# The lo parts of the attention weights made on GpSimd instead of VectorE, in a two-layer decoder step

## The chip, the cores and the metric

The kernel runs on one core of a Trainium2 chip. TensorE multiplies matrices, VectorE and ScalarE work element by element, GpSimd (POOL in the profile) is a further engine that here issues some DMAs, and SyncE issues most DMAs. Each engine takes its instructions in order from its own queue; engines wait for each other by semaphores. The metric is the time of one execution on the device, in microseconds, lower is better.

## The reference, cut to what matters

One step of a two-layer decoder for a prompt of 512 tokens and 8 single-token samples, model width 1024. Layer 0 mixes by pooling, layer 1 by attention within a window of 128 keys. Each layer has a gated feed-forward block before and after its mixer. All is float32. The part that the change touches is the mixer of layer 1:

```python
q = _rope((h @ w_q[j]).reshape(B, T, N_KV_HEADS, GROUP, HEAD_DIM), pos)
out = _window_attention(q, kk, vv, wb, pos0, attn_sinks[j]) @ w_o[j]
x = x + out
```

w_q and w_o are 1024 x 1024. The attention takes softmax over two blocks of 128 keys with a learned sink per head, for 16 heads of 64 and 4 key heads.

## The kernel before

**Split products.** TensorE is fed a rounded format (fp32r) here, and to keep float32 accuracy every operand is written as hi + lo: hi is the operand rounded, lo is what is missing. A product is three matmuls: hi x hi, hi x lo, lo x hi (terms, L410; mm, L413). The tokens are the moving side: 520 columns, as two halves of 260. A weight tile is loaded for each matmul.

**Weight stream.** The class Weights (L97) holds a list of chunks (1 MB loads into the tile raw, three buffers) and of pieces (views of a chunk, mostly 128 x 4 x 128, that is 512 elements a partition). _split (L180) makes a piece ready: ScalarE copies it into wh with rounding (L194), VectorE subtracts to get wl (L195), each from a ring of six buffers. get takes the next piece, prefetch makes pieces up to five ahead of the last one taken, and loads chunks up to two ahead. A raw buffer is free again when the last piece read from it has its wh and wl.

The list for layer 1's mixer is 16 query pieces (four chunks, L305 to L322) and 16 output pieces (four chunks, L323 to L337); numbered 0 to 31 below. The query pieces are views with a gap every 64 elements, the output pieces of 128. The next feed-forward block's pieces follow.

**Attention.** A table of cosines and sines, csq, is loaded into a raw buffer, from ScalarE's queue (L1036, L1037). For each of 8 tiles t of the query, q_part multiplies two pieces; q_evac (L1056) then ropes the result on VectorE (L919 to L923: a product with the cosines, a shuffle, a product with the sines, a sum), and splits it. 16 units (t and half) follow: scores on TensorE, the masked maximum (L1101) and small steps on VectorE, exponentials on ScalarE (L1121), scaling by the denominator on both (L1134, L1136), transposes (L1146) and their split (L245, L246), and the product with the values (L1169). The loop at L1313 interleaves the units with the query products of later tiles, and from turn 12 with the first half of the output product (o_part, L1278), whose second half follows at L1340. load_values (L1294) loads the cached values of the samples into a raw buffer, vc, and writes the samples' own value row into it by a DMA from GpSimd's queue (L1297).

**GpSimd here.** Its queue has the two memsets of qz at the start (L1042), and the DMA of L1297. In the feed-forward blocks it issues accumulating DMAs (L158, L159).

**Order.** Instructions are written in the order of the program text, and the order on each engine is then made by a planner, which runs the program in a timeline of estimated durations (L1449); instructions wrapped in later keep their place relative to each other.

Of the kernel before, what the change touches and what calls it, by code (L numbers as in the profile page):

```python
# [11 lines left out]
F32 = mybir.dt.float32  # L12
# [3 lines left out]
ALU = mybir.AluOpType  # L16
# [80 lines left out]
class Weights:  # L97
# [4 lines left out]
    def __init__(self, nc, rawp, splp, chunks_ahead, ahead):  # L102
        self.nc, self.rawp, self.splp = nc, rawp, splp
        self.ca, self.ahead = chunks_ahead, ahead
        self.chunks, self.items = [], []
        self.nl = self.na = self.ns = self.ng = 0
        self.late = None
        self.pin = lambda ins: ins

    def chunk(self, *dmas):  # L110
        self.chunks.append([list(dmas), None, None])
        return len(self.chunks) - 1
# [67 lines left out]
    def _split(self, i):  # L180
        nc = self.nc
        while self.ns <= min(i, len(self.items) - 1):
            it = self.items[self.ns]
            self.load(it[0])
            self.add_up(it[0])
            src = it[1](self.chunks[it[0]][1])
            n = src.shape[1]
            wh = self.splp.tile([P, 4, P], F32R, tag="wh", name="wh")
            wl = self.splp.tile([P, 4, P], F32R, tag="wl", name="wl")
            dh, dl = wh[:, :n, :], wl[:, :n, :]  # L190
            if len(src.shape) == 4:
                dh = dh.rearrange("p k (e d) -> p k e d", e=2)
                dl = dl.rearrange("p k (e d) -> p k e d", e=2)
            self.pin(nc.scalar.activation(dh, src, AF.Copy))  # L194
            self.pin(nc.vector.tensor_tensor(dl, src, dh.bitcast(F32), op=ALU.subtract))  # L195
            it[2] = (wh, wl)
            held = any(c < it[0] for c, _, _ in self.items[self.ns + 1 : self.ns + 3])
            self.load(it[0] + self.ca - held)
            self.add_up(it[0] + 1)
            self.ns += 1  # L200
# [12 lines left out]
def yoco_step(ctx, tc, ins, outs):  # L213
    nc = tc.nc
# [20 lines left out]
    def pair(tags, shape, dtype=F32R):  # L235

        return tuple(big.tile(shape, dtype, tag=t, name=t) for t in tags)
# [3 lines left out]
    def split(dst, src, scale=None):  # L241

        hi, lo = dst
        if scale is None:
            S.activation(hi, src, AF.Copy)  # L245
            V.tensor_tensor(lo, src, hi.bitcast(F32), op=ALU.subtract)  # L246
        else:
            S.activation(hi, src, AF.Copy, scale=scale)
            V.scalar_tensor_tensor(lo, src, scale, hi.bitcast(F32), op0=ALU.mult, op1=ALU.subtract)

    def later(ins):

        return tc.keep_in_program_order(ins)


    W = Weights(nc, rawp, splp, 2, 5)
# [93 lines left out]
    def gcol(n, k):  # L350
        return gT[:, n * 8 + k : n * 8 + k + 1]
# [12 lines left out]
    def square(k, pool, tag, order=lambda ins: ins):  # L364
        sq = pool.tile([P, TOK], F32, tag=tag, name="sq", bufs=1 if tag == "rp0" else 2)
        S.activation(sq, x[k], AF.Square)
        if k == 0:
            order(V.tensor_copy(acc[:, :TOK], sq))
        else:
            order(V.tensor_tensor(acc[:, :TOK], acc[:, :TOK], sq, op=ALU.add))  # L370
# [259 lines left out]
    def deferred(n, tmp, tag, tags, lst, w=TOK):  # L630


        def f(k):
            z = pair(tags, [P, w])
            split(tuple(a[:, :TOK] for a in z), x[k], gcol(n, k))
            lst.append(z)
            square(k, tmp, tag)

        return f
# [393 lines left out]
    with tc.tile_pool(name="at", bufs=2) as at:  # L1033
# [152 lines left out]
        def q_part(t, h):  # L1186
            if h == 0:
                qb[t] = duo()
            q_half(qb[t], 4 * h)

        later(S.activation(warm, ones[:, 0:1], AF.Exp))
        for h in (0, 1):
            q_part(0, h)
        qq[0] = q_evac(0, qb[0])
# [78 lines left out]
        def o_samples(t):  # L1273
            split(tuple(a[:, SP:TOK] for a in mov5[t]), oS[:, t, :])
# [38 lines left out]
        for n in range(2 * KT + VLAG):  # L1313
# [21 lines left out]
            if n == 13:  # L1335
                for t in range(len(mov5)):
                    o_samples(t)
        later(S.activation(warm, ones[:, 0:1], AF.Silu))
        after_o = deferred(5, at, "rp0", XX, mov6)
        for m in range(KT):  # L1340
            o_part(m, 4, after=after_o)
# [111 lines left out]
```

## Time and profile before

| what | us |
|---|---|
| median of 3 runs (1691.66 to 1692.97) | 1692.24 |
| the profiled execution, its time | 1691.85 |
| its span | 1690.0 |
| query products begin on TensorE | 1143.0 |
| first masked maximum on VectorE | 1163.1 |
| last value product on TensorE ends | 1294.6 |

From 1143 to 1296, busy time of single groups on the engines that share the work:

| engine, line, work | count | us |
|---|---|---|
| ScalarE L1121 exponentials, with reads of their sums | 64 | 49.7 |
| ScalarE L194 wh | 25 | 15.5 |
| ScalarE L1134 scaling | 32 | 14.4 |
| VectorE L1101 masked maximum, with reads of it | 64 | 29.3 |
| VectorE L246 lo of the transposed probabilities (from PSUM) | 32 | 19.7 |
| VectorE L195 wl | 25 | 17.1 |
| VectorE L920, L922, L923 rope products and sum | 24 | 16.7 |
| VectorE L1136 scaling | 32 | 9.8 |

A row of instruction groups gives the line, engine, operation, out and in tiles with their shapes, the count, and then busy time and the mean of one in ns; after a second bar the idle time of the engine just before them, and what ended it. A row in order of time gives start, duration, engine, line, and in brackets the idle time before it with its releaser. On VectorE an instruction's last part overlaps the next one's start, so the busy times add up to a little more than the time they take.

### The profile page before, as it was taken

The numbers are of one execution on the slowest core, as the hardware profiler recorded it, in microseconds if no ns is written. First come the engines' busy times: TensorE is split into PE (matmuls) and PEld (weight loads), VectorE is DVE, ScalarE is ACT, GpSimd is POOL, SyncE is SP. The second block draws the span as 40 slices with busy tenths as digits, with TensorE's granted clock in tenths as the row PEclk, the third lists the DMA queues.
The fourth block names the chain that finished last, engine by engine and source line by source line (L and its number), as shares of the span: only waits on it lengthen the run. The fifth ranks groups of instructions, "written<-read, shape, count | busy, mean of one in ns | idle before, by whom it ended". The sixth has DMA issues, their size and how long they took to land.

```text
span 1690.0 us, 34449 instructions
## 1 busy us (share of the span) xinstructions
PE 1657.5 (98%) x13754; PEld 1642.7 (97%) x13754; DVE 1254.4 (74%) x2452; ACT 903.5 (53%) x1793; POOL 142.3 (8%) x176
## 2 busy tenths in 40 slices
PE   9999999999999999999999999999989999999997
PEld 8999999999999999999999999998879999999996
DVE  6866866887875875888775875888876885785776
ACT  6743643665652652656552652655886653463454
POOL 0101101000101101100101101100000100110100
PEclk9999999999999999999999999999899999999998
DMA  8546745652545855634745845642122554674631
GB/s 214 137 128 142 181 134 136 174 167 80 129 140 129 178 147 130 153 117 129 162 137 125 187 137 127 152 138 71 50 51 76 131 137 131 148 173 132 148 109 52
DMA packets 313327, 224.71 MB, mean 133 GB/s; under 512 B 9152, under 2 KB 289320, under 8 KB 313126
## 3 DMA queue, kind: packets, MB, share of 16 engines
q1 hardware_dynamic: 286416, 176.13, 36.8%
q0 software_dynamic: 22432, 40.26, 14.5%
q10 hardware_dynamic: 4318, 6.12, 1.2%
q8 instruction: 108, 1.77, 0.4%
q14 instruction: 53, 0.43, 0.1%
HBM read 180.11 MB, written 5.04 MB: 110 GB/s over the span
## 4 chain that ended last, share of the span: by engine, by line
PE 90%; DVE 4%; ACT 3%; DMA 1%; issue 1%; DVEq 0%; ACTq 0%
PE ps L443 45%; PE ps L417 41%; ACT sm L1121 1%; PE ps L1169 1%; PE ps L814 1%; DVE wl L195 1%; DMA pr<-in_bands_dram 1%; PE ps L839 1%; DVE sm L1101 1%; DVE xl L246 0%; ACT wh L194 0%; PE ps L1146 0%; PE ps L381 0%; PE ps L698 0%; DMA pr<-in_pool_w_dram 0%
## 5 line engine op out<-in xcount | busy, mean ns | idle before, releaser
L194 ACT ACTIVATE wh<-raw 128x512 fp32r<-128x512 f32 (+1 forms) x736 | 446.3, 621 | 544.8 <-PE ps L417 329.5
L195 DVE TENSOR_TENSOR wl<-raw,wh 128x512 fp32r<-128x512 f32 (+1 forms) x736 | 486.9, 676 | 200.7 <-ACT wh L194 197.2
L443 PE MATMUL ps<-th,wh 128*128 128x260 f32 x1216 | 343.7, 283 | 0.0
L443 PE MATMUL ps<-tl,wh 128*128 128x260 f32 x1216 | 343.1, 282 | 0.0
L443 PE MATMUL ps<-th,wl 128*128 128x260 f32 x1216 | 341.5, 282 | 0.0
L417 PE MATMUL ps<-hh,wh 128*128 128x260 f32 x1376 | 284.3, 285 | 2.3 <-DVE mx L1101 1.0
L417 PE MATMUL ps<-hl,wh 128*128 128x260 f32 x1376 | 283.2, 283 | 0.0
L417 PE MATMUL ps<-hh,wl 128*128 128x260 f32 x1376 | 280.7, 282 | 0.0
L443 PEld LDWEIGHTS ps<-tl,wh 128*128 128x128 f32 x1216 | 229.0, 188 | 0.0
L443 PEld LDWEIGHTS ps<-th,wh 128*128 128x128 f32 x1216 | 228.7, 188 | 0.2 <-ACT sa L523 0.2
L443 PEld LDWEIGHTS ps<-th,wl 128*128 128x128 f32 x1216 | 228.1, 188 | 0.0
L417 PEld LDWEIGHTS ps<-hh,wh 128*128 128x128 f32 x1376 | 213.5, 189 | 4.0 <-DVE mx L1101 1.2
L417 PEld LDWEIGHTS ps<-hl,wh 128*128 128x128 f32 x1376 | 215.2, 189 | 0.1
L417 PEld LDWEIGHTS ps<-hh,wl 128*128 128x128 f32 x1376 | 214.0, 189 | 0.0
L443 PE MATMUL ps<-xh,wh 128*128 128x260 f32 x672 | 188.3, 283 | 0.0
L443 PE MATMUL ps<-xl,wh 128*128 128x260 f32 x672 | 188.2, 283 | 0.0
L443 PE MATMUL ps<-xh,wl 128*128 128x260 f32 x672 | 184.2, 282 | 0.0
L159 POOL DMA_DIRECT2D raw<-raw x76 | 65.5, 862 | 1302.8 <-DMA raw<-in_ffn_w_up_dram 438.9
L417 PE MATMUL ps<-xh,wh 128*128 128x260 f32 x736 | 149.4, 285 | 0.6 <-ACT wh L194 0.6
L417 PE MATMUL ps<-xl,wh 128*128 128x260 f32 x736 | 149.5, 284 | 0.5 <-DVE xl L717 0.5
L417 PE MATMUL ps<-xh,wl 128*128 128x260 f32 x736 | 147.8, 283 | 0.1
L591 DVE TENSOR_TENSOR u<-ps,R 128x520 f32<-128x520 f32 (+1 forms) x99 | 67.2, 681 | 106.3 <-PE ps L417 106.3
(260 smaller groups left out, 2849.1 us busy)
## 6 DMA issues: line engine op xcount, KB each, us to landing
raw<-in_ffn_w_gate_dram SPq DMA_DIRECT2D x87, 512.0 KB, 3.9
raw<-in_ffn_w_up_dram SPq DMA_DIRECT2D x87, 512.0 KB, 5.4
raw<-in_ffn_w_down_dram SPq DMA_DIRECT2D x32, 1024.0 KB, 5.3
raw<-raw POOLq DMA_DIRECT2D x76, 256.0 KB, 3.3
S<-in_ffn_w_up_dram SPq DMA_DIRECT2D x76, 256.0 KB, 5.6
S<-raw POOLq DMA_DIRECT2D x76, 256.0 KB, 4.7
raw<-in_ffn_w_down_dram SPq DMA_DIRECT2D x16, 768.0 KB, 4.9
raw<-in_w_q_dram SPq DMA_DIRECT2D x8, 512.0 KB, 4.0
```

Of the source, the lines that this page charges most:

```text
L159: G.dma_start(blk(raw, 2, 1), blk(raw, 1, 1), accum_op=ALU.add)
L194: self.pin(nc.scalar.activation(dh, src, AF.Copy))
L195: self.pin(nc.vector.tensor_tensor(dl, src, dh.bitcast(F32), op=ALU.subtract))
L417: ins = T.matmul(banks[:, hf, :H], a[:, kk, :], hcols(b, hf), start=(first and i == 0), stop=(last and i == 2),)
L443: T.matmul(bank[:, :H], a[:, kk, :], b, start=(not more and kk == 0 and i == 0), stop=(kk == 3 and i == 2), skip_group_check=more,)
L591: V.tensor_tensor(parts(u), bank[:, hfs[0] : hfs[-1] + 1, :H], parts(R[:, c]), op=ALU.mult)
L814: T.matmul(o, a[:, s], b[:, kk, :], start=(n == 0), stop=(n == 5))
L839: T.matmul(po[:, half * 256 : half * 256 + 256], z[:, tau, c], b, start=(i == 0), stop=(i == len(lst) - 1),)
L1101: ins = V.tensor_tensor_reduce(out=sm[:, e * 256 : (e + 1) * 256], in0=self.pe[e][:, bi * 256 : (bi + 1) * 256], in1=cst[:, mk : mk + 256] ...
L1121: S.activation(part(i), part(i), AF.Exp, scale=r8[:, b : b + 1], bias=nm[:, i : i + 1], accum_out=den[:, i : i + 1],)
L1169: T.matmul(po[:, bi * 256 : (bi + 1) * 256], a, p_[:, kc_], start=(n == 0), stop=(n == 3 * len(kts) - 1),)
```

## The change

A field W.lo names the engine that makes wl. It is VectorE, is set to GpSimd just before the first query product, and set back just before the second half of the output products. The instruction and its operands stay the same.

```diff
@@ -106,6 +106,7 @@
         self.late = None
         self.pin = lambda ins: ins
+        self.lo = nc.vector
@@ -192,7 +193,7 @@
             self.pin(nc.scalar.activation(dh, src, AF.Copy))
-            self.pin(nc.vector.tensor_tensor(dl, src, dh.bitcast(F32), op=ALU.subtract))
+            self.pin(self.lo.tensor_tensor(dl, src, dh.bitcast(F32), op=ALU.subtract))
@@ -1189,6 +1190,8 @@
         later(S.activation(warm, ones[:, 0:1], AF.Exp))
+
+        W.lo = nc.gpsimd
         for h in (0, 1):
             q_part(0, h)
@@ -1336,6 +1339,7 @@
         later(S.activation(warm, ones[:, 0:1], AF.Silu))
+        W.lo = nc.vector
         after_o = deferred(5, at, "rp0", XX, mov6)
         for m in range(KT):
             o_part(m, 4, after=after_o)
```

Which pieces are made while the field names GpSimd follows from the prefetch: a piece is made when it comes within five of the last one taken.

## The prediction

> **What bounds the kernel now.** I read the engine totals first, then the slices, then tables of ten-microsecond windows through attention, then the chain of waits there, and last VectorE's own order of time. Columns of the first view: busy time, share of the span, instructions; in the second, a digit is tenths of a slice.
>
> ```profile
> PE 1657.5 (98%) x13754; PEld 1642.7 (97%) x13754; DVE 1254.4 (74%) x2452; ACT 903.5 (53%) x1793; POOL 142.3 (8%) x176
> ...
> PE   9999999999999999999999999999989999999997
> ...
> PEclk9999999999999999999999999999899999999998
> ```
>
> TensorE is busy 98% of 1690.0 us. The one dent inside the run, in busy time and granted clock, is attention; nothing outside it can be won by lightening VectorE. The windows show what each engine does there (columns: length, PE, PEld, DVE, ACT, POOL busy with counts, granted clock, DMA share, GB/s):
>
> ```profile
> 1160.00:1170.00 10.00, 9.95 (x91) 9.06 (x91) 9.89 (x41) 2.39 (x5) 0.00 (x0) 1.00 0.30 69
> 1170.00:1180.00 10.00, 9.33 (x78) 8.44 (x77) 8.06 (x36) 10.00 (x32) 0.00 (x0) 1.00 0.20 40
> 1180.00:1190.00 10.00, 5.98 (x30) 5.09 (x31) 7.98 (x33) 8.22 (x25) 0.00 (x0) 0.62 0.46 105
> 1190.00:1200.00 10.00, 10.00 (x74) 9.43 (x73) 5.70 (x19) 6.42 (x19) 0.00 (x0) 0.87 0.01 2
> ...
> 1230.00:1240.00 10.00, 6.80 (x47) 6.04 (x47) 8.87 (x33) 7.35 (x22) 0.00 (x0) 0.85 0.45 104
> ...
> 1260.00:1270.00 10.00, 9.77 (x88) 8.78 (x88) 7.28 (x31) 7.38 (x25) 0.00 (x0) 1.00 0.49 107
> 1270.00:1280.00 10.00, 10.00 (x87) 10.00 (x86) 8.54 (x30) 9.73 (x31) 0.00 (x0) 1.00 0.40 107
> ```
>
> Summed over the thirteen windows from 1150 to 1280, TensorE idles 12.8 us of 130; the clock below 1.00 in four windows is worth up to 0.68 of a window, 6.8 us, more. So at most 19.6 us can be won. The order matters: in 1160 to 1170 VectorE is full (9.89) while ScalarE idles (2.39); then ScalarE is full, and then TensorE stalls and its clock falls. The softmax work starts late because VectorE is late. The chain shows what starts VectorE:
>
> ```profile
> 1148.76 0.64 ACT wh L194
> 1149.42 0.70 DVE wl L195
> 1150.15 3.57 DMA csq<-in_consts_dram
> ```
>
> The rope table csq needs a raw buffer. It is the one of the second query chunk, whose last reader is the eighth lo piece at 1149.42. The table's load starts when that piece ends, and VectorE's row tells the rest:
>
> ```profile
> 1149.42 0.69 DVE L195 TENSOR_TENSOR wl<-raw,wh 128x512 fp32r<-128x512 f32 x1 [1.73 <-ACT wh L194]
> ...
> 1153.74 0.70 DVE L920 TENSOR_TENSOR qT<-rp,csq 128x520 f32<-128x520 f32 x1 [2.96 <-DMA csq<-in_consts_dram]
> 1154.36 0.69 DVE L922 TENSOR_TENSOR rp<-rp,csq 128x520 f32<-128x520 f32 x1
> 1154.97 0.69 DVE L195 TENSOR_TENSOR wl<-raw,wh 128x512 fp32r<-128x512 f32 x1
> 1155.57 0.69 DVE L923 TENSOR_TENSOR qT<-qT,rp 128x520 f32<-128x520 f32 x1
> ```
>
> VectorE stands 2.96 us for that table. A lo piece takes 0.69 us, but the next instruction starts 0.60 us after it, so 0.605 us is what one is worth in a full queue.
>
> **Which pieces move.** The first five query pieces are made before the switch, since the prefetch runs five ahead; the first on GpSimd is piece 5. At the switch back 24 pieces have been taken (16 query, 8 output), so pieces up to 28 are made: 24 in all, each 128x512. In VectorE's order they are three before the table (1143.63, 1147.01, 1149.42), five from 1154.97 to 1168.65, nine from 1176.12 to 1227.72, and seven from 1268.00 to 1289.34. No DMA moves engine; the weight loads that wait for a lo piece wait on GpSimd's instead.
>
> **What is removed.** 24 x 0.605 = 14.5 us of VectorE. The last seven are worth nothing: from 1260 TensorE is busy 9.77 and 10.00 of 10, and its work hides them. The first three lie beside the query products at a full TensorE too. The five of the full stretch are worth 5 x 0.605 = 3.0 us. Of the nine in the middle (5.4 us) I count half, 2.7, since the chain there alternates between VectorE and ScalarE.
>
> **What a piece costs on GpSimd.** No row shows it doing such a subtraction. Its nearest rows:
>
> ```profile
> masks.py:199 POOL TENSOR_SCALAR_AFFINE_SELECT ident<-ident 128x128 f32<-128x128 f32 x1 | 0.3, 312 | 0.1
> L1042 POOL MEMSET qz<- 128x64 f32 x2 | 0.2, 151 | 23.8 <-DVE acc L370 23.8
> masks.py:197 POOL MEMSET ident<- 128x128 f32 x1 | 0.2, 204 | 0.3 <-POOLq L1437 0.3
> L1437 POOL MEMSET const-float32-0.0<- 128x1 f32 x1 | 0.1, 99 | 0.2 <-issue 0.2
> ```
>
> Fixed 99 ns. One written stream: (204-99)/128 = 0.82 ns an element. One read and one written: (312-99)/128 = 1.66. So a stream is 0.83, and two read and one written make 2.5 ns: 0.10 + 512 x 2.5 = 1.37 us. Ends: VectorE's own 0.69 below, 0.10 + 2 x 0.85 = 1.80 above (each input costing a whole read and write). I take 1.37. [...]
>
> **The head.** GpSimd's memset of qz waits until 1147.21 and ends by 1147.45, so piece 5 starts then, not at 1143.63. Pieces 5, 6, 7 follow without a gap (their wh are ready at 1143.2, 1146.7, 1149.4): ends at 1148.8, 1150.2, 1151.55. The table's load then starts 1.45 us later than at 1150.1, and the first rope with it. The load is issued from ScalarE's queue, so the exponential table (1.28 us) and piece 8's wh (1152.76) queue behind the same wait; they slip by under a microsecond, and no one needs piece 8 before 1168. With 0.69 us a piece the head would be nothing, with 1.80 it is 2.75.
>
> **Does GpSimd hinder VectorE?** No row has both reading on-chip tensors at once. Ends: nothing, or every VectorE instruction with two on-chip tensor inputs waits out the GpSimd piece. From 1158 to 1190 such instructions (ropes, lo parts of qT, the small nm and es, with the copies and scalings whose 256 elements take 0.265 us) are 20.8 us of 34.4, 60%. The full price is 1.37 x 0.6 = 0.82 a piece; VectorE idles about 15% of 1160 to 1230 (59.2 busy of 70), which takes it to 0.70. I take this end, with the none end kept: GpSimd's instructions that did run beside VectorE (DMA issues, memsets) read no tensor into the engine, so their harmlessness (VectorE's L195 never passes 695 ns) says little. [...]
>
> **The sum.** Full stretch: +1.45 (head) - 3.0 (removed) + 4 x 0.70 (the fifth piece falls into the wait for the table) = +1.25 us. Middle: 9 x (0.70 - 0.605) / 2 = +0.4. Together 1.65 us of later softmax. Every idle microsecond of TensorE came with 6.8/12.8 = 0.5 us of lower clock, so x1.5: +2.5 us. The profiled execution took 1691.85 us (span 1690.0), 0.4 below the median of the runs, 1692.24; I put the 2.5 us on the median: **1694.7**.
>
> **What costs nothing, and its cover.** GpSimd's queue also holds the write of the new value row into vc, which waits for vc's load (issued 1213.41, landed by about 1218.6). Lo pieces 20 on would queue behind it; their wh is not ready before 1223.7, and a piece is made some 14 us before its use (five pieces x 2.87 us of matmul). Without that cover a late vc would stop TensorE one for one. The output chunks' loads start 0.7 us later and still land over ten microseconds early.
>
> **Rivals.**
> *No hindrance, faster.* Full stretch +1.45 - 3.0 = -1.55, middle -2.7, x1.5: -6.4 us, 1685.8. For it: VectorE is demonstrably the full engine ahead of the stall. Against: no row shows the two side by side. With h us of hindrance a piece the sum is 1.5 x (-1.55 + 4h + 4.5(h - 0.605)), so it is faster by over 0.2% from h below 0.24.
> *A long piece, slower.* At 1.80 us the head costs 2.75, hindrance is 1.8 x 0.6 = 1.08: full stretch 2.75 - 3.0 + 4.3 = +4.05, middle 9 x (1.08 - 0.605)/2 = +2.1; 6.2 x 1.5 = +9.3, 1701.5. It decides from about 1.45 us a piece. For it: the strided query views; against: the stream count.
> *The planner.* The program order comes from a timeline estimate in which these pieces now sit on another engine. If it moves the rope or the exps, the big stall (4.0 us idle, 3.8 of clock in 1180 to 1190) may go, 1684, or come twice, 1700.
>
> **Chances.** Forecast 0.44, no hindrance 0.24, long piece 0.26, planner 0.06. A measurement tells about 0.2% (3.4 us) from no change. The forecast's own range is 1692 to 1698: 0.30 within, 0.13 above, 0.01 below. No hindrance: 0.18 faster, 0.06 within; long piece: 0.23 slower, 0.03 within; planner: 0.03 faster, 0.02 slower, 0.01 within. Faster 0.22, same 0.40, slower 0.38. The range 1686 to 1703 leaves out half of the first rival and a quarter of the second.
>
> **What would show it.** GpSimd: 24 subtractions of 1.2 to 1.5 us. The csq load issued near 1151.5. VectorE instructions with two on-chip inputs lengthened, or starting late with the GpSimd piece as releaser, and not those with a PSUM input. The window 1160 to 1170 still full. If instead VectorE's durations stay at 0.69 us and ScalarE's exps start before 1169, the first rival holds and I am wrong in sign.

## The result, and the profile after

The changed kernel takes 1707.04 us (median of 6 runs, 1701.92 to 1708.27) against 1692.58 for the kernel before (median of 6 runs, 1691.66 to 1696.70). The ratio over all runs is 1.007, 95% interval 1.0055 to 1.0085: slower, by some 12 us (the two medians lie 14.5 us apart), and above the range of the prediction. The profiled execution took 1706.35 us, its span is 1704.3.

The page of the changed kernel, totals (busy time, share, instructions), then the 40 slices:

```profile
PE 1665.2 (98%) x13754; PEld 1650.0 (97%) x13754; DVE 1255.3 (74%) x2428; ACT 904.2 (53%) x1793; POOL 174.8 (10%) x200
...
PE   9999999999999999999999999998989999999997
...
PEclk9999999999999999999999999999889999999998
```

POOL has 24 instructions and 32.5 us more. DVE has 24 instructions fewer and yet 0.9 us more busy time. In a full queue one of the 24 was worth 0.605 us of it, because its end overlaps the next start, so the others grew by about 24 x 0.605 + 0.9 = 15.4 us. The dent of attention is wider: two slices at 8 where there was one, and one more at a lower clock.

Spans can't simply be subtracted: the first 40 us differ from one execution to the next, although the instructions there are the same (the second group of row sums on TensorE began at 34.72 us in the kernel before and at 36.71 after; 38.55 in an experiment below). I therefore measure **the stretch**: from TensorE's row sums ahead of attention (L381, product of ones and acc) to the same sums of the block behind it. As one window, in the kernel before and then in the changed one (columns: length, busy time and count of PE, PEld, DVE, ACT, POOL, the clock granted to TensorE as a share of the full one, DMA share, GB/s):

```profile
1148.80:1323.30 174.50, 161.72 (x1324) 151.96 (x1323) 135.12 (x449) 126.81 (x331) 1.42 (x2) 0.96 0.24 61
```

```profile
1152.15:1337.78 185.63, 166.74 (x1324) 156.73 (x1323) 136.56 (x427) 127.14 (x331) 30.96 (x24) 0.93 0.23 58
```

The stretch is 11.1 us longer: 6.1 us of idle TensorE (185.63 - 166.74 = 18.9 against 12.8) and 5.0 us more time for the same 1324 matmul records at a clock of 0.93 in place of 0.96. Behind it all is as before: from the sums at its end to the last ones of the span it is 352.2 us in both. Each kernel has one profiled stretch only, so how far the stretch of one kernel varies between executions is not known.

The windows of the changed kernel that answer to the four shown of before:

```profile
1160.00:1170.00 10.00, 8.03 (x70) 7.15 (x70) 9.60 (x27) 3.11 (x7) 3.85 (x3) 1.00 0.00 0
1170.00:1180.00 10.00, 10.00 (x89) 9.73 (x88) 8.84 (x41) 4.69 (x15) 1.28 (x1) 1.00 0.49 108
1180.00:1190.00 10.00, 5.62 (x47) 4.61 (x47) 8.50 (x28) 8.33 (x27) 4.21 (x3) 0.95 0.15 40
1190.00:1200.00 10.00, 7.69 (x42) 6.87 (x40) 5.38 (x19) 5.78 (x17) 0.00 (x0) 0.54 0.34 67
```

VectorE is nearly as full as before in 1160 to 1170, with no piece left to make there. ScalarE's 10.00 of 1170 to 1180 has become 4.69, because the exponentials come later: at 1176.5 for 1170.6, of which 3.35 is the later start of the stretch; 2.5 us remain. The stall follows, later and longer.

**What happens to one instruction.** Three rows of GpSimd's order of time in the changed kernel, then what VectorE did meanwhile (start, duration):

```profile
1162.55 1.29 POOL L196 TENSOR_TENSOR wl<-raw,wh 128x512 fp32r<-128x512 f32 x1 [1.37 <-ACT wh L195]
1167.73 1.39 POOL L196 TENSOR_TENSOR wl<-raw,wh 128x512 fp32r<-128x512 f32 x1 [3.90 <-ACT wh L195]
1173.31 1.28 POOL L196 TENSOR_TENSOR wl<-raw,wh 128x512 fp32r<-128x512 f32 x1 [4.20 <-ACT wh L195]
```

```profile
1162.60 1.78 DVE L247 TENSOR_TENSOR xl<-qT,xh 128x512 fp32r<-128x512 f32 x1
...
1167.91 1.23 DVE L389 SCALAR_TENSOR_TENSOR nt<-nt,nv 128x5 f32<-128x5 f32 x1
...
1170.78 0.15 DVE L1205 TENSOR_SCALAR rs<-R 128x8 f32<-128x8 f32 x1
1170.85 0.42 DVE L1102 CUSTOM_DVE_ANT_0 sm<-ps,cst 128x256 f32<-128x256 f32 x1
...
1173.26 0.42 DVE L1102 CUSTOM_DVE_ANT_0 sm<-ps,cst 128x256 f32<-128x256 f32 x1
...
1173.60 1.55 DVE L923 TENSOR_TENSOR rp<-rp,csq 128x520 f32<-128x520 f32 x1
```

The step on nt has five elements a row and takes 0.15 us; here it starts at 1167.91, inside a GpSimd piece that ends at 1169.12, and ends at 1169.14. The split xl and the rope product each last until the piece beside them is done, plus a little less than their own length (0.54 us past its end, where a split takes 0.68; 0.56, where a product takes 0.69). The maxima between read one input, ps, from PSUM, where the kernel has TensorE's results. The last of them runs beside the third piece and keeps its 0.42; of all 64 maxima six run beside a piece, and none takes over 0.43. The groups over attention show the same sorting. Kernel before, 1143 to 1312 (after the bar: busy us, mean ns):

```profile
L1101 DVE CUSTOM_DVE_ANT_0 sm<-ps,cst 128x256 f32<-128x256 f32 x64 | 24.0, 419 | 7.9 <-PE ps L1146 4.1 <-PE ps L1088 3.6
L246 DVE TENSOR_TENSOR xl<-ps,xh 128x512 fp32r<-128x512 f32 x24 | 16.4, 685 | 4.8 <-ACT xh L245 4.6
L1136 DVE TENSOR_SCALAR sm<-sm,den 128x256 f32<-128x256 f32 x32 | 9.8, 348 | 0.2
L246 DVE TENSOR_TENSOR xl<-qT,xh 128x512 fp32r<-128x512 f32 x8 | 5.5, 681 | 0.0
L1116 DVE TENSOR_TENSOR nm<-nm,nsinks 128x4 f32<-128x4 f32 x16 | 2.4, 157 | 0.2
```

Changed kernel, the same groups and the piece on GpSimd:

```profile
L1102 DVE CUSTOM_DVE_ANT_0 sm<-ps,cst 128x256 f32<-128x256 f32 x64 | 23.9, 416 | 7.7 <-PE ps L1147 5.6 <-PE ps L1089 2.1
L247 DVE TENSOR_TENSOR xl<-ps,xh 128x512 fp32r<-128x512 f32 x24 | 16.3, 685 | 7.9 <-ACT xh L246 7.8
L1137 DVE TENSOR_SCALAR sm<-sm,den 128x256 f32<-128x256 f32 x32 | 14.6, 498 | 0.2
L247 DVE TENSOR_TENSOR xl<-qT,xh 128x512 fp32r<-128x512 f32 x8 | 7.6, 950 | 0.0
L1117 DVE TENSOR_TENSOR nm<-nm,nsinks 128x4 f32<-128x4 f32 x16 | 5.4, 339 | 0.1
...
L196 POOL TENSOR_TENSOR wl<-raw,wh 128x512 fp32r<-128x512 f32 x24 | 32.2, 1346 | 138.9 <-ACT wh L195 119.1 <-PE ps L1023 19.7
```

The first two groups read PSUM and stay. For the second this run proves little, as none of its 24 meets a piece for longer than 0.2 us; in g1 below eight splits from PSUM do, and none takes over 0.69 us. The other three groups have no input in PSUM, all of it in the on-chip memory that the pieces lie in too (SBUF), and grow by 40 to 120%. Added up row by row over the stretch, the pieces left out, VectorE's instructions take 13.8 us more than in the kernel before. This sum is called **hindrance** below; in the four runs with every piece on VectorE and nothing added on GpSimd (e2, e3, f5, f6) it lies within 0.6 us of zero. In the chain of waits the head now reads:

```profile
1152.82 1.29 POOL wl L196
1154.13 3.58 DMA csq<-in_consts_dram
```

**The second thing that changed** is in the order of time above: the first masked maximum stands right behind rs (L1205), the end of the norm chain (the small steps from nv to rs that turn the row sums into the norm's factors), at 1170.85. In the kernel before it began at 1163.1, in the middle of that chain. The planned orders of the two kernels are the same on SyncE, and on GpSimd but for the pieces; on TensorE, VectorE and ScalarE they differ from the start of attention on.

### The profile page after: what moved, and what is told of

Read it like the earlier page. It is cut to its first block, busy times and chain, and to the rows that moved or that the text cites. A ratio compares the mean times of both kernels' runs of the same rounds, so it can differ in the third digit from the quotient of the medians.

```text
span 1704.3 us, 34466 instructions
## 1 busy us (share of the span) xinstructions
PE 1665.2 (98%) x13754; PEld 1650.0 (97%) x13754; DVE 1255.3 (74%) x2428; ACT 904.2 (53%) x1793; POOL 174.8 (10%) x200
## 4 chain that ended last, share of the span: by engine, by line
PE 91%; DVE 4%; ACT 3%; DMA 1%; issue 0%; ACTq 0%; POOL 0%; DVEq 0%; POOLq 0%
PE ps L444 45%; PE ps L418 42%; ACT sm L1122 1%; PE ps L1170 1%; PE ps L815 1%; DVE sm L1102 1%; PE ps L840 1%; DVE xl L247 1%; DMA xt<-in_x_prompt_dram 0%; PE ps L382 0%; DVE sm L1137 0%; PE ps L1147 0%; ACT xh L246 0%; DVE wl L196 0%; DVE rp L922 0%
## 5 line engine op out<-in xcount | busy, mean ns | idle before, releaser
L196 DVE TENSOR_TENSOR wl<-raw,wh 128x512 fp32r<-128x512 f32 (+1 forms) x712 | 470.6, 676 | 196.8 <-ACT wh L195 193.5
```

The costliest lines, as they stand in the source:

```text
L196: self.pin(self.lo.tensor_tensor(dl, src, dh.bitcast(F32), op=ALU.subtract))
```

## The experiments

All hold the same computation unless said. "Order held" means that the program is planned once with the pieces on one engine, and built a second time with them on another, the instructions of PE, ACT, DVE and SP then tied to the sequence of the first plan:

```diff
+    LO[0], EXTRA[0] = "vector", None
+    with tile.TileContext(nc, schedule_with_timeline_sim=True) as tc:
+        yoco_step(tc, args, outs)
...
+    LO[0], EXTRA[0] = "gpsimd", set()
...
+                tc.add_manual_dep(
+                    i,
+                    prev[e].name,
+                    mybir.DependencyInfo(mybir.DependencyClass.NoSync, mybir.DependencyReason.DATA),
```

The last table puts the runs side by side; ratios are against runs of the kernel before on the same chip, with 95% intervals, and the stretch is that of one profiled execution each. That execution was the slowest of its kernel's runs in e2 and f4, and among the faster ones in e1, so where ratio and stretch differ the ratio is the safer measure.

### Order or engine: e1 and e2

e1 has the pieces on GpSimd in the order of the kernel before (edit above; the tie of the first maxima, of which more below, is left off when it is built). e2 is the opposite: pieces on VectorE, order of the changed kernel ("gpsimd" in the first plan, "vector" in the second).

> The 24 lo pieces on GpSimd, all other instructions on TensorE, VectorE, ScalarE and the SyncE queue in the order of the kernel before; unit 0's masked maxima are not tied to the instruction traced in front of them. Theory A (GpSimd's reads hold up VectorE): VectorE's two-input instructions and its scalings lengthen by about 15 us in all, as in the changed kernel, and the time is 1700 to 1707. Theory B (the loss comes from the new order, which the moved tie brings about): the lengthening is there too, but the 14.5 us taken off VectorE pay for it, and the time is within 3 us of before, 1690 to 1696. If GpSimd did not hinder at all it would be 1686.

> All lo pieces on VectorE, but TensorE, VectorE, ScalarE and the SyncE queue in the order of the changed kernel (the 24 pieces placed by the planner in between). Theory A: no hindrance, so the time is near before, 1690 to 1696. Theory B: most of the loss is in the order, 1701 to 1708, or more, since VectorE now also carries the 14.5 us of pieces.

e1: 1.0027 (1.0014 to 1.004), stretch +3.3 us. e2: 1.0039 (1.0024 to 1.0055), stretch +8.0. The sum of the stretches is 11.2, the changed kernel has 11.1; the ratios add up to 1.0066 against 1.007. So the change did two things, and the order costs its price with every piece on VectorE. By the stretch it is the larger of the two. By the ratios it is 6.6 us against 4.6, and the intervals overlap, so which is larger is not settled. e1's median, 1698.87 us, lies between the ranges of its two theories: GpSimd does hinder (12.7 us), and the time taken off VectorE pays for only part of it. What TensorE waited for in the stretch, longest first (us in total, times, longest); kernel before, then e2:

```profile
PE ps L1169 <- ACT xh L245: 4.5, 2, 2.5
PE ps L1169 <- DVE mx L1101: 1.7, 2, 1.5
PE ps L1169 <- DVE xl L246: 1.5, 3, 1.0
```

```profile
PE ps L1174 <- ACT xh L250: 4.7, 2, 3.5
PE ps L422 <- ACT oT L1186: 2.0, 2, 1.6
PE ps L1174 <- DVE oS L1272: 1.8, 1, 1.8
```

The large stall on the split probabilities stays. New are waits late in attention: the output product (L422) for the attention's result oT, and the values (L1174) for the samples' oS; both are 0.2 us or less in the kernel before.

### Where the order comes from: e3 and e4

In the program text the maxima of the first tile (two units) are wrapped in later, which keeps an instruction behind the one traced just ahead of it on its engine. With the pieces on VectorE that one is a wl piece; without them it is rs, the end of the norm chain. e3 ties the maxima to rs in the kernel before; e4 takes the tie out of the changed kernel:

```diff
                         if self.t == 0:
-                            later(ins)
+                            tc.add_manual_dep(
+                                ins.ins,
+                                rs8_made.ins.name,
+                                mybir.DependencyInfo(mybir.DependencyClass.NoSync, mybir.DependencyReason.DATA),
+                                reason="pin",
+                            )
```

```diff
-                        if self.t == 0:
-                            later(ins)
```

> The kernel before, lo pieces on VectorE, with unit 0's masked maxima tied behind the instruction that makes rs8, as they come to be tied when the lo pieces leave VectorE's list; the planner is free otherwise. Theory A: the tie is harmless, 1690 to 1696. Theory B: the first softmax starts after the whole chain of the norm (first maximum near 1170 instead of 1163), and the time is 1699 to 1708.

> The changed kernel without the tie on unit 0's masked maxima (in the kernel before, taking it away changes no engine's order). Theory A: 1700 to 1707, as changed. Theory B: within 4 us of before, 1688 to 1697, with the first maximum back near 1163 to 1166.

e3: 1.0000 (0.9989 to 1.0011), stretch +0.8. e4: 1.0015 (1.0002 to 1.0027), stretch +2.6. The tie alone costs nothing; without it the changed kernel gets back 8.5 of its 11.1 us of stretch, and its median, 1695.03, is back within 4 us of before. In these four plans, then, the bad order came only with both: a list of VectorE without the pieces, and the tie that then lands on rs. How is not shown. The planner was free in e3 and e4, and on VectorE some 170 instructions of e3 and 250 of e4 stand at another place than in the kernel before (240 in the changed kernel), so a new order is not slow as such. Nor does the late start of the maxima itself lose the time: counted from the start of the stretch they begin at 16.9 us in e3 and at 14.3 before, and e3 loses nothing by it.

### Hindrance and relief, each alone: f1 and f2

Both with the order held. f1 leaves the pieces on VectorE and gives GpSimd a like subtraction beside each; f2 leaves them out but for one element a partition, and has GpSimd fill wl with zeros, so next to nothing is read in their place:

```diff
+            if self.more is not None and EXTRA[0] is not None:
+                extra = nc.gpsimd.tensor_tensor(self.more, wh.bitcast(F32), wh.bitcast(F32), op=ALU.subtract)
```

```diff
+                nc.gpsimd.tensor_tensor(dl[one], src[one], dh[one].bitcast(F32), op=ALU.subtract)
+                EXTRA[0].add(nc.gpsimd.memset(wl.bitcast(F32), 0.0).ins.name)
```

> Every subtraction stays on VectorE, in the order of the kernel before on all engines; for each of the 24 pieces GpSimd makes one more subtraction of the same size beside it, wh less wh into a tile of its own, which nobody reads. The load of csq has its old place. Theory (GpSimd's two-input work shuts VectorE out): with nothing of VectorE's removed, the instructions lengthened in the changed kernel (scaling 348 to about 500 ns, xl from qT 681 to about 950) are lengthened here too, VectorE's busy time goes up by 12 to 18 us, and the first exps start about 4 us later (1.9 us in e1, less 0.6 for its later table, plus 3.0 for the five pieces that are not removed here). At 1.5 us of time for each that is 6 us, ratio 1.0035, up to 1.006 if the middle adds its part. Rival (the loss in e1 comes from when the pieces are ready, not from a shared way to memory): no VectorE row longer, ratio 1.000.

> The order of the kernel before on PE, ACT, DVE and SP. The 24 second parts are left out: in place of each subtraction GpSimd subtracts one element a partition, so that the waits stay what they were in e1, and then fills wl with zeros, which reads nothing. This prices the relief of VectorE without GpSimd's reading. Theory (only reading both inputs shuts VectorE out): scaling stays near 348 ns and xl from qT near 681, the first exps start 2 to 3 us earlier than in the kernel before, and at 1.5 us each with up to 2.7 us more in the middle the ratio is 0.995 to 0.998. Second theory (any GpSimd write shuts it out for its length): the same rows go up by about a third of what they did in the changed kernel, ratio 0.998 to 1.000. Rival (VectorE is not what is late there): rows unchanged and ratio 1.000.

f1: 1.0045 (1.0026 to 1.0063), stretch +6.2. VectorE's busy time in the stretch rises from 135.12 to 145.24 with the same 449 instructions: 10.1 us, under the 12 to 18 that were expected. The added subtraction reads wh twice and is shorter than a piece where nothing holds it up (1.04 us at the least, a piece 1.27), though its mean is 1.27 too: the first of three that take 4.05 us together, for one, starts at 1179.13, beside a piece of VectorE that runs from 1179.02 to 1179.71. The first exponentials start 2.7 us late where about 4 were expected. f2: 0.999 (0.9975 to 1.0005), stretch -3.1; its first exponentials start 0.7 us earlier, not the 2 to 3 expected. The sum of the two stretches, 3.1, is near e1's 3.3: with the order held, the move is a relief worth some 3 us, bought with a hindrance that costs some 6. The match is closer than the pricing, as f1 holds VectorE up for 10.3 us and e1 for 12.7. The stretch of e1, then of f2:

```profile
1149.33:1327.09 177.76, 162.25 (x1325) 153.16 (x1324) 135.03 (x427) 126.67 (x331) 31.72 (x24) 0.95 0.24 60
```

```profile
1154.33:1325.74 171.41, 159.77 (x1324) 150.45 (x1323) 123.40 (x427) 127.01 (x331) 19.21 (x46) 0.97 0.24 61
```

VectorE has 22 instructions less than before in both. In f2 that takes 11.7 us off its busy time, in e1 nothing (135.03 against 135.12): the hindrance eats all that the move takes off. Groups of f1 and then of f2:

```profile
L1145 DVE TENSOR_SCALAR sm<-sm,den 128x256 f32<-128x256 f32 x32 | 12.4, 429 | 0.2
L929 DVE TENSOR_TENSOR qT<-rp,csq 128x520 f32<-128x520 f32 x8 | 6.8, 850 | 3.0 <-DMA csq<-in_consts_dram 3.0
...
L203 POOL TENSOR_TENSOR more<-wh 128x512 f32<-128x512 f32 x24 | 30.5, 1270 | 113.5 <-ACT wh L200 107.1 <-ACT es L1138 6.0
```

```profile
L1147 DVE TENSOR_SCALAR sm<-sm,den 128x256 f32<-128x256 f32 x32 | 10.1, 359 | 0.2
L257 DVE TENSOR_TENSOR xl<-qT,xh 128x512 fp32r<-128x512 f32 x8 | 5.5, 682 | 0.0
L1127 DVE TENSOR_TENSOR nm<-nm,nsinks 128x4 f32<-128x4 f32 x16 | 2.4, 157 | 0.2
...
L206 POOL MEMSET wl<- 128x512 f32 x24 | 12.9, 536 | 1.4
```

GpSimd fills for 12.9 us in f2, and no two-input instruction of VectorE is longer for it: the rope product at 1169.63, for one, begins inside a fill and takes its usual 0.70 us. The scalings are, by 11 ns in the mean (693 at the most, where 348 is usual), and so is one copy into qz (476 ns, where 166 is usual). So in this run the fill, which has no input, left the two-input instructions alone, where f1's subtraction takes the rope product from 691 ns in the kernel before to 850. Why a fill holds up some scalings and a copy is not shown.

### Which pieces: f3 and f4

Order held; f3 has only pieces 5 to 12 on GpSimd, f4 only 13 to 28 (the bounds are 0 and 12 in f3, 13 and 28 in f4):

```diff
+            lo = self.lo if 13 <= self.ns - self.n0 <= 28 else nc.vector
+            self.pin(lo.tensor_tensor(dl, src, dh.bitcast(F32), op=ALU.subtract))
```

> The order of the kernel before; only pieces 5 to 12 (the three of the head and the five of VectorE's full stretch) are made on GpSimd, 13 to 28 stay on VectorE. In e1 the exps of the first four units were late by 1.9, 2.0, 2.0 and 2.7 us, those of the fifth by 4.2, and from there to the end the lateness stayed at 3.3 to 4.2. Theory (all of e1's loss is made by these eight pieces): ratio 1.0027 as in e1, lateness 3 to 4 us from the fifth unit on. Rival (each of the 24 pieces costs alike): a third of e1's, 1.0009.

> The other part of e1 alone: the order of the kernel before, pieces 5 to 12 on VectorE, 13 to 28 on GpSimd. Theory (all of e1's loss is made by the first eight): ratio 1.000, within 0.001, though scaling and xl from qT are lengthened in this part too. Rival (each piece costs alike): 1.0018. Third (hindrance spared only there, so relief shows): below 0.999.

f3: 1.0026 (1.0013 to 1.0039), stretch +2.1. f4: 1.0017 (1.0005 to 1.0028), stretch +4.1. The theory that the first eight make all of e1's loss falls: the last sixteen cost something too. f3 has e1's ratio as that theory says, but its exponentials are only 1.1 us late from the fifth unit on, where e1's are 2.8 to 4.1. The two stretches add up to 6.1 us where e1 has 3.3; the ratios, 1.0043 against 1.0027, do not tell that excess from noise. If each piece cost a 24th of e1's loss, f3 would be at 1.0009, below its interval. What a piece costs VectorE differs by the instruction it meets (in the changed kernel a maximum beside one keeps its 0.42 us, a step on nt goes from 0.15 to 1.23), and one piece taken away may shift the later meetings. No run separates this, so I don't put a price on single pieces.

### Which half of the order: f5 and f6

Pieces on VectorE, one order up to the ninth unit (about 1225 us), the other from there; the two orders have placed the same instructions by then:

```diff
+    first, then = plan(given, "gpsimd"), plan(given, "vector")
+    early = set(first[:CUT])
+    return first[:CUT] + [n for n in then if n not in early]
```

f6 has "vector" and "gpsimd" the other way round.

> All subtractions on VectorE, as in e2. PE, ACT, DVE and SP are held to the changed kernel's order up to the ninth unit of attention (about 1225 us in the kernel before), and to the order of the kernel before from there. Theory (the new order loses in its second half: in e2 the exps, less the 5.5 us by which its attention started late, were behind those of the kernel before by 0.3 to 1.0 us in units 1 to 12, then by 2.5, 4.2, 4.5 and 9.0 in units 13 to 16): ratio at most 1.001. Rival (the first maxima, put behind the norm chain, set all that follows): ratio 1.004 as in e2.

> The other half: the order of the kernel before up to the ninth unit, the changed kernel's order from there, all subtractions on VectorE. Theory (the second half loses): ratio 1.003 to 1.004, the last four units' exps late by 2 to 9 us as in e2, and idle TensorE with a low clock between 1250 and 1285. Rival (the start loses): 1.000.

f5: 1.0019 (1.0005 to 1.0033), stretch +3.9. f6: 1.0033 (1.0021 to 1.0046), stretch +6.8. In f6 the exponentials of the last four units are late by 1.1, 2.7, 3.4 and 7.8 us, much as in e2. By the stretch the second half is the worse one, as expected (the two intervals overlap), but the first half is not free: in f5 the lateness is below 1 us up to the 13th unit and then grows to 3.8 under the old order. The two add up to 10.7 us of stretch where e2 has 8.0, so the halves are not independent. So the maxima behind the norm chain are not the whole of the order's cost; in e2 and f6 most of the lateness comes up in the last four units. Which of the changed places counts was not tried, and the cause there stays open.

### Held for one whole instruction: g1 and g2

Each piece in four subtractions of 128x128; g1 with the order held (compare e1), g2 as the changed kernel without the tie (compare e4):

```diff
+                for k in range(n):
+                    c = slice(k, k + 1)
+                    ins = nc.gpsimd.tensor_tensor(dl[:, c], src[:, c], dh[:, c].bitcast(F32), op=ALU.subtract)
```

> As e1 (the order of the kernel before, 24 pieces on GpSimd), but each piece is made by four subtractions of 128x128 in place of one of 128x512. In e1 single small VectorE instructions stood up to 1.26 us (nm 158 ns as a rule, 1259 at the most), about one GpSimd piece. Theory (GpSimd holds the way to memory for one whole instruction, and VectorE comes in between two): no VectorE instruction is lengthened by more than about 0.45 us, nm stays under 0.6 us, the VectorE time lost falls by half or more, and of the hindrance (6.2 us in f1, net of its start) at most half is left: ratio 0.999 to 1.001 where e1 had 1.0027. Rival (the two share the way at a rate, or VectorE waits for the whole queue of GpSimd): lengthening and ratio as in e1, or a little worse, since four instructions cost some 0.3 us more than one.

> As e4 (the changed kernel without the tie of the first maxima, order left to the planner), with each piece made by four subtractions of 128x128. e4 had 1.0015. Theory (held for one whole instruction): 0.999 to 1.001, the lengthening cut by half or more against e4. Rival: 1.0015 or above.

g1: 0.9999 (0.9987 to 1.001), stretch -0.65. g2: 0.9995 (0.9982 to 1.0007), stretch +0.7. The small step nm in e1 and then in g1 (ns, least, median, most):

```profile
L1121 DVE TENSOR_TENSOR nm<-nm,nsinks x16: 132/158/1259, 1172.8 to 1276.4; 128x4 f32<-128x4 f32 x16
```

```profile
L1128 DVE TENSOR_TENSOR nm<-nm,nsinks x16: 132/161/425, 1173.7 to 1274.4; 128x4 f32<-128x4 f32 x16
```

The longest nm falls from 1259 to 425 ns, where a piece takes 1.27 us at the least and a quarter 460 ns in the median. VectorE's busy time in the stretch is 128.66 in g1 (135.03 in e1):

```profile
1151.19:1325.04 173.85, 159.10 (x1325) 149.96 (x1324) 128.66 (x427) 126.86 (x331) 46.25 (x90) 0.98 0.25 61
```

The hindrance went from 12.7 to 6.3 us, the half that was expected, and the loss went with it. In g2 it went from e4's 13.7 to 8.6 us, less than the half expected. GpSimd's own time rose, to 4 x 0.540 = 2.16 us a piece from 1.346 in the changed kernel: 0.8 more, where some 0.3 had been expected. No run beat the kernel before beyond its interval: quarters make the move free, not a gain.

| run | pieces on | order | ratio | stretch, us | against before | clock |
|---|---|---|---|---|---|---|
| before | VectorE | before | | 174.5 | | 0.96 |
| after | GpSimd | new | 1.007 | 185.6 | +11.1 | 0.93 |
| e1 | GpSimd | before | 1.0027 | 177.8 | +3.3 | 0.95 |
| e2 | VectorE | new | 1.0039 | 182.5 | +8.0 | 0.93 |
| e3 | VectorE | planned anew, tied | 1.0000 | 175.3 | +0.8 | 0.94 |
| e4 | GpSimd | planned anew, untied | 1.0015 | 177.1 | +2.6 | 0.95 |
| f1 | VectorE, and more on GpSimd | before | 1.0045 | 180.7 | +6.2 | 0.93 |
| f2 | left out, filled | before | 0.999 | 171.4 | -3.1 | 0.97 |
| f3 | 5 to 12 on GpSimd | before | 1.0026 | 176.6 | +2.1 | 0.96 |
| f4 | 13 to 28 on GpSimd | before | 1.0017 | 178.6 | +4.1 | 0.92 |
| f5 | VectorE | new, then before | 1.0019 | 178.4 | +3.9 | 0.92 |
| f6 | VectorE | before, then new | 1.0033 | 181.3 | +6.8 | 0.94 |
| g1 | GpSimd, quarters | before | 0.9999 | 173.9 | -0.65 | 0.98 |
| g2 | GpSimd, quarters | planned anew, untied | 0.9995 | 175.2 | +0.7 | 0.95 |

## Why the prediction was wrong

**The step that failed is the order.** The prediction took the sequence of instructions as given and left a change of it to a rival with 0.06, which named the right symptom (the stall comes again, 1700 us) and no cause. By e2 the new order costs 8.0 of the 11.1 us of stretch, and 1.0039 of the 1.007 by the ratios; without it (e1) the median is 1698.87 us, inside the stated range. The program text held what brought the order about: the first tile's maxima are pinned to whatever is traced ahead of them on VectorE, the change takes that neighbour away, and the planner's timeline has the pieces on another engine besides. That both were needed I could not have known from the text, but that the pin would land elsewhere, I could. Why this order is slow, beyond the last units being late, stays open.

**With the order held, the number comes close, in part by luck.** The forecast was made for e1's case and said +2.5 us, 1.0015; e1 measured 1.0027 (1.0014 to 1.004), with the forecast at the interval's edge. The sign and the kind were right; the terms below were not.

**The relief was too big.** Removed work: 3.0 in the full stretch and 2.7 in the middle, times 1.5, would be 8.6 us; f2 gave 3.1 of stretch and 0.999, an interval that leaves 8.6 us out. Hindrance: (4 x 0.70 + 4.5 x 0.70) x 1.5 = 8.9; f1 gave 6.2 of stretch and 1.0045, an interval that holds 8.9 us, so this term is not shown to be too big. What a microsecond taken off VectorE is worth was taken too high. Relief and the two costs, hindrance and head, nearly cancelled, and so the small sum survived.

**Length of a piece:** 1.37 us forecast; 1.346 in the mean, its own waits included, and 1.27 at the least. About right, and the rival of the long piece falls twice: the piece isn't longer, and in g1 it takes 2.16 us at no loss. What counted in e1 and g1 was the length of one instruction (nm at most 1259 and 425 ns), not that of the piece.

**Hindrance a piece:** 0.70 forecast; 13.8 us over the 22 pieces in the stretch of the changed kernel is 0.63, in e1 12.7 over 22 is 0.58. No row of the kernel before shows a hindrance: 0.70 was the upper of two ends, my estimate. The kind was right too: two on-chip inputs (xl from qT 681 to 950 ns), not the maxima with one from PSUM (419 and 416), with copies (into qz, 166 to 222) and scalings (348 to 498) as counted.

**The head** was oversized: 1.45 us forecast. Two pieces ran ahead of the memsets of qz, not behind them; the csq load was issued 2.0 us after the row sums began (1154.13 against 1152.15) where it had been 1.35 (1150.15 against 1148.80), so 0.6 later.

**The clock:** 1.5 us for each idle one. Here 6.1 us of idle came with 5.0 at the lower clock, a factor of 1.8.

**The first rival,** no hindrance, is refuted by the rows; f2, the nearest run to that case, is worth about 0.1% rather than its 0.4%.

## What to carry to other kernels

Before moving work to another engine, look for instructions whose place in the order is pinned to their neighbour in the text: the pin moves when the neighbour leaves, and here the new order cost at least about as much as the move itself. GpSimd work that reads on-chip memory was not free here beside a VectorE that works on two inputs from SBUF: it gave back about what it took off (135.03 us of VectorE in e1, 135.12 before). If it must run there, try it in short instructions: four in place of one took the hindrance from 12.7 to 6.3 us here, and the ratio from 1.0027 to 0.9999. Price relief and hindrance by a run of each alone, as their difference is small and either is easy to oversize.

## What the hardware showed beyond that

GpSimd waited too: in g1 its quarters take 460 ns in the median, and the longest of them, 991 ns, lies beside a rope product of VectorE (0.70 us); in the changed kernel a piece that starts at 1159.66, inside the rope product of 1159.31 to 1160.01, takes 1.51 us where 1.29 is the median. And an execution's first 40 us scatter by up to 3.9 us with the same instructions (second row sums at 34.6 to 38.6 us over fourteen profiled executions). That may be part of the reason why single runs of the unchanged kernel ranged from 1690.84 to 1699.13; what makes up the rest, and what causes the scatter, was not looked for.
